# A hybrid GLA/MLA decoder trunk: another rule for the order of its instructions, and MLA's rotary scores as two stacked 128-row products with the mask on TensorE

## The chip, the cores and the metric

The kernel runs on one core of one Trainium2 chip. The metric is the device time of one execution in microseconds (us). TensorE (PE) multiplies matrices, VectorE (DVE) and ScalarE (ACT) work elementwise, GpSimd (POOL) helps, SyncE (SP) issues most of the transfers from HBM.

## What is computed

Two layers; layer 0 mixes tokens with gated linear attention (GLA), layer 1 with multi-head latent attention (MLA). Each layer is a feed-forward half-step, the mixer with four heads of attention to a memory of 256 tokens, and a second feed-forward half-step. All is float32, 512 tokens of width 1024.

```python
for i in range(DEPTH):                                   # DEPTH = 2
    x = x + 0.5 * swiglu(rmsnorm(x, ...), ...)           # d_ff 2816
    h = rmsnorm(x, mix_norm[i])
    # i = 0: gated linear attention, 4 heads;  i = 1: MLA, 8 heads
    o, o_mem = token_mixer(h), memory_cross_attention(q_mem, rmsnorm(mem), ...)
    x = x + concat([o, o_mem]) @ w_out[i]
    x = x + 0.5 * swiglu(rmsnorm(x, ...), ...)

def mla_attention(c_q, c_kv, k_r, ...):
    q  = (rmsnorm(c_q)  @ w_uq ).reshape(B, S, 8, 128 + 64)
    kv = (rmsnorm(c_kv) @ w_ukv).reshape(B, S, 8, 128 + 128)
    q_nope, q_rope = rmsnorm(q[..., :128]), apply_rope(rmsnorm(q[..., 128:]), cos, sin)
    k_nope, v      = rmsnorm(kv[..., :128]), kv[..., 128:]
    k_rope = apply_rope(rmsnorm(k_r), cos, sin)          # one key of 64 for all heads
    s = (q_nope @ k_nope.T + q_rope @ k_rope.T) * 192 ** -0.5
    return softmax(where(causal, s, -inf)) @ v           # in blocks of 128 queries
```

## The kernel before

**Numbers as two parts.** The weights and most activations go to TensorE as a high part, rounded to the format fp32r, and a low part, the rest; a product is then three fp32r products (`mm3`: high by high, high by low, low by high). The profile prints these as f32 too; they are the ones whose operands are tiles `wh` and `wl` (the parts of a weight). ACT makes the high part of a weight (`wh<-raw`), DVE the low part (`wl<-raw,wh`). Products inside the two attentions of a mixer, with operands in tiles `t` only, are mostly plain float32: such a product is one row in the program and two records in the trace.

**Flows and their order.** The program has no order written out by hand. Every piece of work is a Python generator (a flow) that yields one instruction after the other; `Flows.run` takes, again and again, the flow whose next instruction could start first, and emits that instruction to its engine. When it could start is worked out from a table of prices (`Engine.price`: a duration and a latency for each operation) and from the times at which the tiles' blocks were written and read. Among equal starts the lower `rank` goes first: 2 for the trunk (all weight products of TensorE in their fixed order), 1 for most helpers, 0 for the urgent ones (attention chains, copies out of PSUM), and for the splitting of weights -1 or 3, as few or enough weights lie ready. So the order on each engine follows from the prices; the time on the chip does not enter it.

**MLA.** After the latents (`latents`, one for each of four token blocks) and the memory's projections, four pairs of heads follow. For each pair the trunk projects keys and values, then queries, from the latents. `query` copies 384 columns of a block out of PSUM (two heads of 128, two rotary parts of 64) and sums their squares; `queries` makes the inverse roots with `newton_rsqrt`, 13 DVE instructions on 16 columns, of which most read what the one ahead wrote; it scales the blocks, rotates the rotary parts on POOL (`rotate`), and transposes three blocks of 128 for each token block. The two heads' rotary parts share one block: head 0 in rows 0 to 63, head 1 in rows 64 to 127. `keys` does the same for the keys, and `rope_key` makes the one rotary key, written twice, in rows 0 to 63 and 64 to 127.

`attend` takes one head. For each block `j` of 128 queries it makes scores of `n = 128 (j + 1)` columns, with two float32 products into one bank:

```python
yield T.matmul(ps[:, :n], lhsT=st["q"][i][:, sl], rhs=st["k"][i][:, :n], start=True, stop=False)
yield T.matmul(ps[:, :n], lhsT=st["q"][2][rp, sl], rhs=kr["t"][rp, :n], start=False, stop=True)
```

The second, over the 64 rows `rp` of its head, is the rotary product: 8 heads by 4 blocks, 32 in all. In `attention` DVE then adds the causal mask to the last 128 columns (`ps<-ps,cm`), takes the maximum, ACT takes the exponential, DVE the reciprocal and the scaling; four transposes at most, a copy by ACT, and the products with the values end the block's chain. At most two blocks of a head run at the same time.

Of the kernel before, what the change touches and what calls it, by code (L numbers as in the profile page):

```python
# [9 lines left out]
F32 = mybir.dt.float32  # L10
# [39 lines left out]
for _part in (  # L50
# [3 lines left out]
    (("rows", QR + KVR + 2 * ROPE), ("cmask", P), ("cos", NJ * 32), ("sin", NJ * 32), ("invn", 3), ("invq", 16)),  # L54
# [67 lines left out]
class Engine:  # L122
# [19 lines left out]
    def price(self, method, kw, outs, ins):  # L142
# [22 lines left out]
class Flows:  # L165
# [11 lines left out]
    def used(self, name, lo, hi):  # L177
        return max([0.0] + [d.get((name, b), 0.0) for d in (self.wr, self.rd) for b in range(lo // BLOCK, hi // BLOCK)])
# [45 lines left out]
    def start(self, op):  # L224
        t = self.clock.get(op.eng, 0.0)
        for r in op.reads:
            t = max(t, self.wr.get(r, 0.0))
        for w in op.writes:
            if op.eng != "PE":
                t = max(t, self.wr.get(w, 0.0))  # L230
            t = max(t, self.rd.get(w, 0.0))
        return t

# [30 lines left out]
    def run(self):  # L264
        while True:
# [12 lines left out]
            (at, _, _), f = best  # L278
# [6 lines left out]
            for w in op.writes:  # L285
                self.wr[w] = max(self.wr.get(w, 0.0), end + op.lat)
# [3 lines left out]
def _emit(tc, ctx, xT, memT, wflat, sizes, cst, out):  # L290
# [816 lines left out]
    def attention(scores, blocks, value, o, mask=None):  # L1107
# [265 lines left out]
    def rotate(dst, src, tabs, n):  # L1373
# [7 lines left out]
        yield G.tensor_tensor(out=dst[:, :, 0:32], in0=a, in1=b, op=ALU.subtract)  # L1381
        yield G.tensor_tensor(out=a2, in0=t1, in1=s1, op=ALU.mult)
        yield G.tensor_tensor(out=b2, in0=t2, in1=c2, op=ALU.mult)
        yield G.tensor_tensor(out=dst[:, :, 32:64], in0=a2, in1=b2, op=ALU.add)
        done(tmp)

    def mla(l, nrm, nxt):
# [6 lines left out]
        yield from rope_tables(rt)  # L1394
        spawn(mem_prep(l, mem.mp))
# [41 lines left out]
        def rope_key():  # L1437
# [10 lines left out]
            kr["t"] = yield tt()  # L1448
            yield A.copy(out=kr["t"], in_=ps)
# [14 lines left out]
        def query(st, j, ps):  # L1464
# [6 lines left out]
            yield V.tensor_reduce(out=ss[:, 4 * j : 4 * j + 2], in_=heads(sq[:, :256], 2), op=ALU.add, axis=AX.X)  # L1471
            yield V.tensor_reduce(out=ss[:, 4 * j + 2 : 4 * j + 4], in_=heads(sq[:, 256:384], 2), op=ALU.add, axis=AX.X)
# [4 lines left out]
        def queries(st):  # L1477
            for f in st["f"]:
                yield f
            ss, rc = st["ss"], small(16)  # L1480
            yield V.tensor_tensor(out=ss, in0=ss, in1=C("invq"), op=ALU.mult)
            yield from rsqrt(rc, ss, 1.0, 16)
            st["q"] = []
            for _ in range(3):
                st["q"].append((yield tt()))
            q0, q1, qr = st["q"]
            for j in range(NJ):
                qn = st["raw"][j]
                for c0, c1, dd, cc in ((0, 256, NOPE, 4 * j), (256, 384, ROPE, 4 * j + 2)):
                    q3 = heads(qn[:, c0:c1], 2)  # L1490
                    yield V.tensor_tensor(out=q3, in0=q3, in1=rc[:, cc : cc + 2].unsqueeze(2).to_broadcast([P, 2, dd]),
                                          op=ALU.mult)
                tabs = [rt[i][:, j, :].unsqueeze(1).to_broadcast([P, 2, 32]) for i in range(4)]
                yield from rotate(heads(qn[:, 384:512], 2), heads(qn[:, 256:384], 2), tabs, 64)
            for j in range(NJ):
                qn = st["raw"][j]
                pt = yield bank()
                for i, c0 in enumerate((0, 128, 384)):
                    yield T.transpose(out=pt[:, i * P : (i + 1) * P], in_=qn[:, c0 : c0 + P], identity=ident)
                done(qn)  # L1500
                sl = slice(j * P, (j + 1) * P)
                for i in range(2):
                    yield A.activation(out=st["q"][i][:, sl], in_=pt[:, i * P : (i + 1) * P], func=AF.Identity, scale=qns)
# [302 lines left out]
```

## Time and profile before

| | |
|---|---|
| median of three runs | 2018.34 us |
| lowest and highest of them | 2017.01 and 5475.93 us |
| the profiled execution | 2016.53 us, of which the span is 2014.7 us |
| PE, busy share of the span | 99% |
| DVE, ACT, POOL | 78%, 49%, 2% |
| granted clock of TensorE | 1.00 |
| HBM | 189.05 MB read, 95 GB/s over the span |

The profile shows one execution, from the first instruction to the last (the span); 1.8 us of the execution lie around it. All instructions carry the line 138 of a helper that emits them, so groups are told apart by tile names and shapes: `ps` a PSUM bank, `t` a working tile, `s` a small one, `cs` the first block of constants (the identity for transposes stands there), `cm` the constants of a mixer (the mask). By its instructions the span falls into the feed-forward of layer 0 (to about 365 us), GLA (to 622), the two feed-forwards between the mixers (to 1390), MLA with its output projection (to about 1640) and the last feed-forward.

### The profile page before, as it was taken

The page shows a single profiled execution, that of the slowest core. Times are in us where ns is not written, and L with a number is a line of the kernel's source. Part 1 is how long each engine was busy: PE and PEld are TensorE (multiplying, and loading weights), DVE is VectorE, ACT ScalarE, POOL GpSimd, SP SyncE. Part 2 cuts the span into 40 slices and gives each one's busy share as a digit, 9 for nine tenths or more (in the row PEclk, how much of TensorE's full clock was granted, in tenths as well). Part 3 has the DMA queues.
Part 4 walks back from the last instruction along what each step waited for, and adds up shares of the span by engine and source line. Part 5 has one row for each costly group of instructions (what it writes and reads, how often), then busy time and mean ns, then how long its engine had stood idle before and what let it go on. Part 6 is the DMA issues. An engine that isn't in the chain of part 4 may idle for free.

```text
span 2014.7 us, 32006 instructions
## 1 busy us (share of the span) xinstructions
PE 1999.7 (99%) x12862; PEld 1796.6 (89%) x12862; DVE 1578.5 (78%) x2573; ACT 978.3 (49%) x1574; POOL 48.4 (2%) x121
## 2 busy tenths in 40 slices
PE   9999999999999999999999999999999999999999
PEld 8999998878987899999899999989877779998997
DVE  8977786548776998678799777865887669987782
ACT  6543444444442664445565444444576456543451
POOL 0000000000000000000000000010031100000000
PEclk9999999999999999999999999999999999999999
DMA  5333333313212133323323333333210212332231
GB/s 180 108 108 102 105 105 112 108 63 105 74 57 79 64 97 114 115 86 104 126 96 105 105 105 100 101 115 111 87 45 32 84 43 84 105 128 92 95 126 63
DMA packets 55589, 193.22 MB, mean 96 GB/s; under 512 B 6160, under 2 KB 7824, under 8 KB 55440
## 3 DMA queue, kind: packets, MB, share of 16 engines
q1 hardware_dynamic: 55152, 189.92, 28.6%
q8 instruction: 101, 1.65, 0.3%
q10 hardware_dynamic: 288, 1.26, 0.2%
q14 instruction: 48, 0.39, 0.1%
HBM read 189.05 MB, written 2.10 MB: 95 GB/s over the span
## 4 chain that ended last, share of the span: by engine, by line
PE 87%; DVE 9%; ACT 2%; issue 1%; DMA 0%; POOL 0%; SPq 0%; ACTq 0%; DVEq 0%; POOLq 0%
PE ps L138 87%; DVE t L138 5%; DVE wl L138 2%; DVE s L138 2%; ACT t L138 1%; ACT wh L138 1%; DMA raw<-wflat 0%; DVE raw L138 0%; DVE x L138 0%; POOL t L138 0%; SPq L138 0%; DVE ps L138 0%; DVE rs L138 0%; ACTq L138 0%; DVEq L138 0%
## 5 line engine op out<-in xcount | busy, mean ns | idle before, releaser
L138 PE MATMUL ps<-t,wh 128*128 128x256 f32 (+1 forms) x6880 | 1528.0, 318 | 2.8 <-ACT wh L138 1.7
L138 PEld LDWEIGHTS ps<-t,wh 128*128 128x128 f32 x6880 | 1141.1, 191 | 96.0 <-issue 7.2
L138 PE MATMUL ps<-t,wl 128*128 128x256 f32 (+1 forms) x3440 | 1091.1, 317 | 0.1
L138 PEld LDWEIGHTS ps<-t,wl 128*128 128x128 f32 x3440 | 655.5, 191 | 45.6 <-issue 3.0
L138 ACT CAST wh<-raw 128x1024 fp32r<-128x1024 f32 (+2 forms) x358 | 368.6, 1031 | 483.8 <-PE ps L138 357.1
L138 DVE TENSOR_TENSOR wl<-raw,wh 128x1024 fp32r<-128x1024 f32 (+2 forms) x358 | 428.4, 1199 | 114.3 <-ACT wh L138 113.6
L138 DVE TENSOR_TENSOR t<-t 128x512 f32<-128x512 f32 (+3 forms) x514 | 306.5, 618 | 13.1 <-ACT t L138 8.4
L138 ACT CAST wh<-t 128x1024 fp32r<-128x1024 f32 x126 | 132.4, 1051 | 185.5 <-PE ps L138 98.9
L138 PE MATMUL ps<-wh,t 128*128 128x256 f32 (+3 forms) x928 | 214.9, 321 | 0.0
L138 DVE TENSOR_TENSOR wl<-t,wh 128x1024 fp32r<-128x1024 f32 x126 | 153.7, 1220 | 48.9 <-ACT wh L138 48.8
L138 DVE SCALAR_TENSOR_TENSOR x<-ps,x 128x512 f32<-128x512 f32 x160 | 109.8, 686 | 104.7 <-PE ps L138 104.6
L138 ACT COPY t<-ps 128x512 f32<-128x512 f32 (+3 forms) x262 | 138.8, 534 | 65.1 <-PE ps L138 58.5
L138 PEld LDWEIGHTS ps<-wh,t 128*128 128x128 f32 x928 | 155.1, 190 | 9.6 <-issue 2.2
L138 DVE TENSOR_TENSOR t<-ps,t 128x512 f32<-128x512 f32 (+2 forms) x191 | 122.6, 645 | 50.3 <-PE ps L138 36.0
L138 PE MATMUL ps<-wl,t 128*128 128x256 f32 (+3 forms) x464 | 148.2, 319 | 0.0
L138 PE MATMUL ps<-t 128*128 128x128 f32 (+6 forms) x760 | 139.7, 328 | 0.8 <-ACT t L138 0.4
L138 ACT CAST t<-t 128x256 fp32r<-128x256 f32 (+1 forms) x196 | 95.3, 509 | 78.8 <-DVE t L138 78.5
L138 PEld LDWEIGHTS ps<-t 128*128 128x128 f32 (+1 forms) x760 | 97.9, 190 | 30.4 <-issue 15.9
L138 DVE SCALAR_TENSOR_TENSOR t<-t 128x512 f32<-128x512 f32 (+1 forms) x168 | 106.0, 636 | 16.9 <-ACT t L138 16.2
L138 DVE TENSOR_TENSOR t<-t,raw 128x1024 f32<-128x1024 f32 x84 | 102.2, 1217 | 0.1
L138 ACT ACTIVATE t<-t 128x512 f32<-128x512 f32 x124 | 76.3, 629 | 48.1 <-DVE t L138 47.8
L138 PEld LDWEIGHTS ps<-wl,t 128*128 128x128 f32 x464 | 88.3, 190 | 4.9 <-issue 0.9
(76 smaller groups left out, 786.4 us busy)
## 6 DMA issues: line engine op xcount, KB each, us to landing
raw<-wflat SPq DMA_DIRECT2D x342, 512.0 KB, 3.3
raw<-wflat SPq DMA_DIRECT2D x12, 192.0 KB, 2.3
x<-xT SPq DMA_DIRECT2D x8, 256.0 KB, 5.6
t<-memT SPq DMA_DIRECT2D x8, 256.0 KB, 3.6
out<-x SPq DMA_DIRECT2D x8, 256.0 KB, 2.0
raw<-wflat SPq DMA_DIRECT2D x4, 448.0 KB, 3.3
cm<-cst ACTq DMA_DIRECT2D x1, 640.0 KB, 3.9
cm<-cst ACTq DMA_DIRECT2D x1, 585.5 KB, 4.2
```

What stands on the lines that cost most here:

```text
L138: return Op(self.name, lambda: real(*args, **kw), cost, _places(ins), _places(outs), lat)
```

## The change

It has two halves.

**The order.** ACT is priced 95 ns more for each pointer operand and for an accumulated sum, POOL higher. An instruction that reads what the same engine wrote (not on PE) counts no latency any more; before, it counted the latency whatever the engine. And a flow's start is handicapped by 60 ns for each rank above 0 when the next flow is chosen.

**MLA.** Each head's rotary query of 64 columns is split into a high and a low part, which lie side by side, so that their transpose is one tile of 128 rows (`st["qr"]`, high in rows 0 to 63, low in 64 to 127). The rotary key, twice 64 rows as before, is split into a high tile and a low tile. The rotary score is then two fp32r products of 128 rows, by the key's high tile and by its low tile. The mask is a third fp32r product, of an identity and the mask in fp32r (`exact`, made once), on the last 128 columns; DVE's add goes. In `query` one sum over six groups of 64 takes the place of two sums; in `queries` one scaling the place of two, and the nope heads' sums are made from two halves each and written twice (three small instructions); `rotate` issues its four products ahead of the difference and the sum. Four blocks instead of three are transposed for each token block, and the copies behind the transposes take both heads in one instruction.

```diff
         if self.name == "ACT":
-            return 100 + 0.833 * n, 130
+            pointers = sum(_is_ap(kw.get(k)) for k in ("scale", "bias"))
+            return 100 + 0.833 * n + 95 * pointers + 95 * _is_ap(kw.get("accum_out")), 130
         if self.name == "POOL":
-            return 100 + 2.2 * n, 200
+            return 100 + 2.8 * n, 250
...
         for r in op.reads:
-            t = max(t, self.wr.get(r, 0.0))
+            t = max(t, self.written(r, op))
...
+    def written(self, r, op):
+        at, lat, eng = self.wr.get(r, (0.0, 0.0, None))
+        return at if eng == op.eng and eng != "PE" else at + lat
...
-                    k = (self.start(f[3]), f[0]() if callable(f[0]) else f[0], f[1])
+                    rank = f[0]() if callable(f[0]) else f[0]
+                    k = (self.start(f[3]) + 60 * max(rank, 0), rank, f[1], self.start(f[3]))
...
-            if mask is not None:
-                sl = slice(j * P, (j + 1) * P)
-                yield V.tensor_tensor(out=ps[:, sl], in0=ps[:, sl], in1=mask, op=ALU.add)
...
-            kr["t"] = yield tt()
-            yield A.copy(out=kr["t"], in_=ps)
+            kr["t"] = yield from pair()
+            yield from split(ps, *kr["t"])
...
-            yield V.tensor_reduce(out=ss[:, 4 * j : 4 * j + 2], in_=heads(sq[:, :256], 2), op=ALU.add, axis=AX.X)
-            yield V.tensor_reduce(out=ss[:, 4 * j + 2 : 4 * j + 4], in_=heads(sq[:, 256:384], 2), op=ALU.add, axis=AX.X)
+            yield V.tensor_reduce(out=ss[:, 6 * j : 6 * j + 6], in_=heads(sq[:, :384], 6), op=ALU.add, axis=AX.X)
...
+                qh, ql = (heads(qn[:, 256:], 2)[:, :, i * ROPE : (i + 1) * ROPE] for i in range(2))
+                yield from rotate(ql, heads(qn[:, 256:384], 2), tabs, 64)
+                yield A.copy(out=qh.bitcast(F32R), in_=ql)
+                yield V.tensor_tensor(out=ql, in0=ql, in1=qh, op=ALU.subtract)
...
-                for i, c0 in enumerate((0, 128, 384)):
-                    yield T.transpose(out=pt[:, i * P : (i + 1) * P], in_=qn[:, c0 : c0 + P], identity=ident)
+                yield from transposes(pt, qn)
...
-                yield T.matmul(ps[:, :n], lhsT=st["q"][2][rp, sl], rhs=kr["t"][rp, :n], start=False, stop=True)
+                for part in range(2):
+                    yield T.matmul(ps[:, :n], lhsT=st["qr"][:, i * S + j * P : i * S + n], rhs=kr["t"][part][:, :n],
+                                   start=False, stop=False, skip_group_check=True)
+                yield T.matmul(ps[:, sl], lhsT=identr, rhs=maskr, start=False, stop=True, skip_group_check=True)
```

Two places show how the instructions stand now. The first is PE, where the scores of the first pair of heads begin. Before: bank 14697 holds head 0's first block, 14698 its second, 14699 and 14700 those of head 1; `t_13090` is the rotary key.

```order
L138 MATMUL ps_14697<-t_14243,t_9731 128x128
L138 MATMUL ps_14697<-t_13090,t_14216 128x128
L138 MATMUL ps_14698<-t_14243,t_9731 128x256
L138 MATMUL ps_14698<-t_13090,t_14216 128x256
L138 MATMUL ps_14699<-t_14275,t_14147 128x128
L138 MATMUL ps_14699<-t_13090,t_14216 128x128
L138 MATMUL ps_14700<-t_14275,t_14147 128x256
L138 MATMUL ps_14700<-t_13090,t_14216 128x256
```

Now, for head 0's first two blocks (banks 14685 and 14686): `t_13414` and `t_13709` are the key's high and low tile, `t_13107` holds the identity and the mask.

```order
L138 MATMUL ps_14685<-t_14265,t_14368 128x128
L138 MATMUL ps_14685<-t_13414,t_14369 128x128
L138 MATMUL ps_14685<-t_13709,t_14369 128x128
L138 MATMUL ps_14685<-t_13107 128x128
L138 MATMUL ps_14686<-t_14265,t_14368 128x256
L138 MATMUL ps_14686<-t_13414,t_14369 128x256
L138 MATMUL ps_14686<-t_13709,t_14369 128x256
L138 MATMUL ps_14686<-t_13107 128x128
```

Two rows for each block have become four, of which three are fp32r. The second place is DVE in `latents`, where the inverse roots of the four token blocks are made, each in small tiles of its own. Before, three of them took turns (13427 and 13428, 13433 and 13434, 13444 and 13445):

```order
L138 SCALAR_TENSOR_TENSOR s_13428<-s_13427 128x3
L138 SCALAR_TENSOR_TENSOR s_13445<-s_13444 128x3
L138 SCALAR_TENSOR_TENSOR s_13433<-s_13434,s_13433 128x3
L138 TENSOR_TENSOR s_13428<-s_13428,s_13426 128x3
L138 TENSOR_TENSOR s_13445<-s_13445,s_13443 128x3
L138 SCALAR_TENSOR_TENSOR s_13434<-s_13433 128x3
L138 SCALAR_TENSOR_TENSOR s_13427<-s_13428,s_13427 128x3
L138 SCALAR_TENSOR_TENSOR s_13444<-s_13445,s_13444 128x3
```

Now the first block's root runs through by itself, with one weight's low part between:

```order
L138 TENSOR_TENSOR s_13432<-s_13432,s_13430 128x3
L138 SCALAR_TENSOR_TENSOR s_13431<-s_13432,s_13431 128x3
L138 SCALAR_TENSOR_TENSOR s_13432<-s_13431 128x3
L138 TENSOR_TENSOR s_13432<-s_13432,s_13430 128x3
L138 SCALAR_TENSOR_TENSOR s_13431<-s_13432,s_13431 128x3
L138 TENSOR_TENSOR wl_13418<-raw_13240,wh_13417 128x1024
L138 SCALAR_TENSOR_TENSOR s_13432<-s_13431 128x3
L138 TENSOR_TENSOR s_13432<-s_13432,s_13430 128x3
L138 SCALAR_TENSOR_TENSOR s_13403<-s_13432,s_13431 128x3
```

Nearly every row now reads what the row ahead of it wrote. Counted over the whole order of DVE, that holds for 450 of 2538 instructions now and for 358 of 2575 before; 65 of the 92 more stand between the 348th and the 372nd weight's low part, which the trace of before has from about 1400 to 1516 us. The order of the weights' transfers on SP is the same, and so is the trunk's on PE.

More of the change, by code (lines that the diff above doesn't have):

```diff
@@ L177, in used @@
     def used(self, name, lo, hi):
-        return max([0.0] + [d.get((name, b), 0.0) for d in (self.wr, self.rd) for b in range(lo // BLOCK, hi // BLOCK)])
+        keys = [(name, b) for b in range(lo // BLOCK, hi // BLOCK)]
+        return max([0.0] + [self.rd.get(k, 0.0) for k in keys] + [sum(self.wr[k][:2]) for k in keys if k in self.wr])
     def done(self, *tiles):
@@ L1104, in _emit, with attention @@
     xqs = const.tile([P, 2], F32, name="xqs")
-    def attention(scores, blocks, value, o, mask=None):
+    def attention(scores, blocks, value, o):
         po = yield bank(1)
@@ L1479, in queries @@
                 yield f
[L1480 to L1486, printed above, removed]
+            ss, rc = st["ss"], sm.tile([P, 24], F32, tag="s6", name="s6", bufs=8)
+            two = ss.rearrange("p (j b) -> p j b", j=NJ)[:, :, :4].rearrange("p j (h b) -> p j h b", h=2)
+            sums = small(8)
+            yield V.tensor_tensor(out=sums.rearrange("p (j h) -> p j h", j=NJ), in0=two[:, :, :, 0], in1=two[:, :, :, 1],
+                                  op=ALU.add)
+            for b in range(2):
+                yield V.tensor_scalar_mul(out=two[:, :, :, b], in0=sums.rearrange("p (j h) -> p j h", j=NJ), scalar1=0.5)
+            v, y, t = (sm.tile([P, 24], F32, tag="s6", name="s6", bufs=8) for _ in range(3))
+            yield from newton_rsqrt(rc, ss, 1.0 / ROPE, v, y, t)
+            st["q"] = yield Take("d", F32, 0)
+            st["qr"] = yield Take("d", F32R, 0)
             for j in range(NJ):
                 qn = st["raw"][j]
[L1489 to L1492, printed above, removed]
+                q3 = heads(qn[:, :384], 6)
+                yield V.tensor_tensor(out=q3, in0=q3, in1=rc[:, 6 * j : 6 * j + 6].unsqueeze(2).to_broadcast([P, 6, ROPE]),
+                                      op=ALU.mult)
                 tabs = [rt[i][:, j, :].unsqueeze(1).to_broadcast([P, 2, 32]) for i in range(4)]
-                yield from rotate(heads(qn[:, 384:512], 2), heads(qn[:, 256:384], 2), tabs, 64)
+                qh, ql = (heads(qn[:, 256:], 2)[:, :, i * ROPE : (i + 1) * ROPE] for i in range(2))
+                yield from rotate(ql, heads(qn[:, 256:384], 2), tabs, 64)
+                yield A.copy(out=qh.bitcast(F32R), in_=ql)
+                yield V.tensor_tensor(out=ql, in0=ql, in1=qh, op=ALU.subtract)
             for j in range(NJ):
@@ L1522, in keys @@
             yield from rsqrt(rc, st["ks"], 1.0 / NOPE, 8)
-            st["k"] = []
-            for _ in range(2):
-                st["k"].append((yield tt()))
+            st["k"] = yield Take("d", F32, 0)
             for j in range(NJ):
@@ L1532, in keys @@
                 sl = slice(j * P, (j + 1) * P)
-                for i in range(2):
-                    yield A.activation(out=st["k"][i][:, sl], in_=pt[:, i * P : (i + 1) * P], func=AF.Identity,
-                                       scale=C("kn"))
+                yield A.activation(out=heads(st["k"], 2)[:, :, sl], in_=heads(pt[:, : 2 * P], 2), func=AF.Identity,
+                                   scale=C("kn"))
                 done(pt)
@@ L1780, in _pack_consts @@
     put("invn", np.broadcast_to(np.array([1.0 / QR, 1.0 / KVR, 1.0 / ROPE], np.float32), (P, 3)))
-    put("invq", np.broadcast_to(np.tile(np.array([1 / NOPE, 1 / NOPE, 1 / ROPE, 1 / ROPE], np.float32), 4), (P, 16)))
     return c
```

32 lines of the change are left out of this document (18 added, 14 removed).

## The prediction

> **What bounds the kernel now.** I read the page's first part, then the busy time by stage, then what ends the waits in the stage that changes.
>
> ```profile
> span 2014.7 us, 32006 instructions
> PE 1999.7 (99%) x12862; PEld 1796.6 (89%) x12862; DVE 1578.5 (78%) x2573; ACT 978.3 (49%) x1574; POOL 48.4 (2%) x121
> ```
>
> PE is busy 1999.7 of 2014.7 us: 15.0 us idle are all that a better order could give back of what the page calls idle. The stages, with PE's busy time as the second number and DVE's as the fourth:
>
> ```profile
> 365.00:622.00 257.00, 256.26 (x1535) 214.83 (x1535) 177.79 (x370) 107.87 (x187) 2.04 (x4) 1.00 0.23 77
> 622.00:1390.00 768.00, 766.76 (x5151) 712.24 (x5150) 627.62 (x809) 373.05 (x522) 5.89 (x8) 1.00 0.31 103
> 1700.00:2014.00 314.00, 310.39 (x2112) 288.86 (x2110) 236.34 (x275) 134.41 (x167) 0.00 (x0) 1.00 0.31 100
> ...
> 1400.00:1495.00 95.00, 90.04 (x525) 78.15 (x524) 85.38 (x324) 61.31 (x159) 22.22 (x53) 1.00 0.27 81
> 1495.00:1640.00 145.00, 143.79 (x768) 107.48 (x768) 96.81 (x281) 78.75 (x218) 16.95 (x50) 1.00 0.15 48
> ```
>
> In the feed-forwards between the mixers PE idles 1.2 of 768 us, in GLA 0.7 of 257. There the time is that of the trunk's products, which the change leaves as they are; DVE has 140 us to spare in the 768, so a moved weight split or copy stays covered. The last row of feed-forward idles 3.6 us, mostly the end. One stretch stands out: the opening of MLA, 1400 to 1495 us, where PE idles 5.0 us while DVE is busy 85.4 of 95. The chain of work through it and one of its waits:
>
> ```profile
> by line: PE ps L138 36.4%; DVE s L138 24.6%; DVE wl L138 12.3%; DVE t L138 9.3%; issue 5.9%; ACT t L138 4.2%; ACT wh L138 3.2%; POOL t L138 3.2%; DVE ps L138 0.9%; ACTq L138 0.1%; POOLq L138 0.0%; DVEq L138 0.0%
> ...
> 1477.20 0.41 PE L138 MATMUL ps<-cs,t 128*128 128x128 f32 x2 [1.33 <-DVE t L138]
> ```
>
> Nearly half of that chain (24.6 + 12.3 + 9.3 + 0.9%) is DVE, and PE stands 1.33 us before a transpose that DVE's scaling of the keys releases. So two prices matter: what TensorE's products in MLA cost, and what DVE needs in MLA's opening.
>
> **PE: the rotary product that goes.** These are the 32 products over 64 rows, two records each, from 1480 to 1630 us:
>
> ```profile
> L138 PE MATMUL ps<-t 64*128 64x512 f32 x16 | 9.0, 641 | 0.0
> L138 PE MATMUL ps<-t 64*128 64x384 f32 x16 | 7.3, 535 | 0.0
> L138 PE MATMUL ps<-t 64*128 64x256 f32 x16 | 5.6, 428 | 0.0
> L138 PE MATMUL ps<-t 64*128 64x128 f32 x16 | 3.9, 322 | 0.0
> ...
> 1499.44 1.44 PE L138 MATMUL ps<-t 128*128 128x128 f32 x4
> 1500.81 0.33 PE L138 MATMUL ps<-cs,t 128*128 128x128 f32 x1
> ```
>
> Together 25.8 us busy. Busy time counts the drain of a product, over which the next may run, so it can be too much; the timeline's group tells. Its four records are two short ones of 128 columns and one rotary product of 512 (the group prints its first shape), and the next group starts 1.37 us after it. With 0.12 us for each short one (below), 1.13 us are left for the product, as 9.0 / 8 = 1.13. So the drain is not covered here, and I take **-25.8 us**. The other end: an fp32r product of 512 lasts 0.39 us and the next starts after 0.23 (next rows), so at most 0.16 us of each is covered, 32 x 0.16 = 5.1, which leaves -20.7.
>
> **PE: what comes.** Starts of neighbouring fp32r products, of 512, 384 and 256 columns:
>
> ```profile
> 1478.61 0.39 PE L138 MATMUL ps<-wl,t 128*128 128x512 f32 x1
> 1478.84 0.62 PE L138 MATMUL ps<-wh,t 128*128 128x512 f32 x2
> ...
> 1481.93 0.34 PE L138 MATMUL ps<-wl,t 128*128 128x384 f32 x1
> 1482.11 0.52 PE L138 MATMUL ps<-wh,t 128*128 128x384 f32 x2
> ...
> 1300.22 0.28 PE L138 MATMUL ps<-t,wl 128*128 128x256 f32 x1
> 1300.34 0.40 PE L138 MATMUL ps<-t,wh 128*128 128x256 f32 x2
> ```
>
> That is 0.23, 0.18 and 0.12 us. No row has an fp32r product of fewer than 256 columns, and 48 of the new ones have 128 (16 rotary, 32 mask). They are bounded by
>
> ```profile
> L138 PE MATMUL ps<-ones,t 128*128 128x1 f32 x20 | 2.4, 237 | 0.0
> L138 PE MATMUL ps<-t 128*128 128x128 f32 x176 | 27.4, 283 | 0.0
> L138 PE MATMUL ps<-cs,t 128*128 128x128 f32 x180 | 30.5, 276 | 2.5 <-ACT t L138 1.8 <-DVE t L138 0.5
> ```
>
> Even one column costs 2.4 / 20 = 0.12 us, as much as 256 columns of fp32r, so 0.12 is the lower end. The upper end is plain float32 of this width: two records of 27.4 / 176 = 0.156, 0.31 us. I take 0.12, since 256 columns of the same format already cost no more. The sum: 16 x (0.23 + 0.18 + 0.12 + 0.12) = 10.4 for the rotary products and 32 x 0.12 = 3.8 for the mask, **+14.2 us**; by the upper end 48 x 0.19 = 9.1 more. Sixteen more transposes, at 30.5 / 180 = 0.17, are **+2.7 us**. PE's own work: -25.8 + 14.2 + 2.7 = **-8.9 us**, with ends -8.9 and -20.7 + 14.2 + 9.1 + 2.7 = +5.3. PE is the bound through this stage (143.8 of 145 us), so I count all of it.
>
> [...]
>
> ```profile
> 438.87 0.70 PE L138 MATMUL ps<-t 64*128 64x256 f32 x4
> 439.50 0.50 PE L138 MATMUL ps<-t,wh 128*128 128x512 f32 x1
> ```
>
> Two products of 256 columns in the two halves take 0.63 us from start to next start; in MLA one takes 5.6 / 8 = 0.70. If MLA's two heads paired up like that, half of 25.8 would have been saved already, and PE's work would change by -12.9 + 14.2 + 2.7 = +4.0. But in the order of before a full-height product stands between any two rotary ones, and their busy rows show no pairing. [...]
>
> **DVE and ACT.**
>
> ```profile
> L138 DVE TENSOR_TENSOR ps<-ps,cm 128x128 f32<-128x128 f32 x32 | 9.5, 295 | 9.4 <-PE ps L138 9.0
> L138 DVE TENSOR_TENSOR t<-t,s 128x256 f32<-128x256 f32 x20 | 8.9, 458 | 0.1
> L138 DVE TENSOR_TENSOR t<-t,s 128x128 f32<-128x128 f32 x12 | 4.1, 338 | 0.0
> L138 DVE TENSOR_REDUCE s<-t 128x2 f32<-128x256 f32 x15 | 6.2, 411 | 1.5 <-ACT t L138 1.5
> L138 DVE TENSOR_REDUCE s<-t 128x2 f32<-128x128 f32 x8 | 2.2, 276 | 0.0
> L138 DVE TENSOR_REDUCE s<-ps 128x1 f32<-128x384 f32 x8 | 4.4, 553 | 0.1
> L138 ACT ACTIVATE t<-ps,qns 128x128 f32<-128x128 f32 x32 | 10.2, 386 | 8.3 <-PE ps L138 8.1
> L138 ACT ACTIVATE t<-ps,s 128x256 f32<-128x256 f32 x24 | 11.4, 479 | 5.1 <-DVE s L138 5.0
> ```
>
> The mask's 32 adds, 9.5 us, leave DVE, and 0.3 us leaves each block's chain. Joined sums save 0.41 + 0.28 - 0.55 = 0.14 us for each of 16 blocks, 2.2; joined scalings 0.46 + 0.34 - 0.58 (extended by 0.12 for each 128 columns) = 0.22, 3.5. The new subtraction costs about 0.34 a block, 5.4; the wider copy out of PSUM and three small instructions for each pair about 4. So DVE is about 6 us lighter over MLA, but the mask falls late: before the first scores, at about 1486 us, it is about even. ACT's joined copies save 2 x 0.39 - 0.48 = 0.29 us, 32 times (queries and keys), 9 us, less 16 casts of about 0.3. I cost these at nothing for the end, since PE covers them from 1495 on; where cover fails, a chain is 0.3 us shorter for the mask, and a query block about 0.6 longer for the cast and the subtraction.
>
> **The order.** What the new prices leave out can be seen in four rows of DVE's timeline:
>
> ```profile
> 1475.37 0.15 DVE L138 TENSOR_TENSOR s<-s 128x8 f32<-128x8 f32 x1
> 1475.44 0.27 DVE L138 TENSOR_REDUCE s<-t 128x2 f32<-128x128 f32 x1
> ...
> 1480.75 0.17 DVE L138 SCALAR_TENSOR_TENSOR s<-s 128x16 f32<-128x16 f32 x1
> 1480.95 0.17 DVE L138 TENSOR_TENSOR s<-s 128x16 f32<-128x16 f32 x1
> ```
>
> A small instruction is followed after 0.07 us by one that does not need its result, and after 0.20 by one that does. The old price had a latency for the second case and put other work between; the new one does not, and 92 more instructions stand right behind the one whose result they read, 65 of them between 1400 and 1516 us. At 0.13 us that is 8.5 us of DVE in the stretch where DVE is 90% busy, and queued behind them are the weights' low parts, the scalings and so PE's transposes. DVE idles 9.6 us there, which absorbs some, and the first block of each kind is ready sooner. I take a third of 8.5 for PE, **+2.8 us**, with ends 0 and 8.5. The handicap of 60 ns lets PE wait up to 0.12 us for an urgent helper; better prices for ACT place helpers nearer to their operands. Both work in the mixers alone; their balance I put at nothing, and the gain at no more than the idle of MLA, 5.0 + 1.2 = 6.2 us.
>
> **The sum**, against the profiled execution's 2016.53 us (span 2014.7): -8.9 + 2.8 = -6.1, **2010.4 us**. The median of the three runs is 2018.34 and the lowest 2017.01, so the profiled one is a usual one.
>
> **The rivals.**
> - *The order repays.* MLA's idle time goes, as chains finish sooner and nothing is lost to the tighter rows: 2016.5 - 8.9 - 6.2 = 2001.4. For it speaks that PE waits for helpers there and that ACT's rows with pointers (0.386 us for 128 columns) lie above their old price; against it DVE's load.
> - *DVE's opening gets slower.* All 92 tight pairs reach PE, 92 x 0.13 = 12.0 us: 2016.5 - 8.9 + 12.0 = 2019.6, slower than before. Place: latents to the first scores, 1400 to 1495 us. It decides once more than 8.9 of the 12.0 us arrive at PE, which needs the opening's DVE slack to be gone.
> - *The narrow products run as float32*, so the change does not do there what it says: 2010.4 + 9.1 = 2019.5. No row excludes it.
> [...]
>
> **How the numbers follow.** Forecast 0.50, order repays 0.22, DVE's opening 0.13, narrow products 0.13, pairing 0.02. The range reaches from the first rival less 3 us for the end of PE's own waits that no row calls idle to the two slower ones and 3.5 us for both of them in part: 1998 to 2023. Two per cent of the median, about what a measurement of this kernel can tell from no change, are 40 us. No case comes near: faster than 1978 would need more than all idle time and the whole rotary product, slower than 2059 several times the loss of any rival. I leave 0.01 and 0.02 for what I have not seen, and 0.97 within.
>
> **What will show it.** The 64-row shapes of MLA are gone, and PE's groups of `ps<-t` with 128 rows grow by 48 records of 128 columns that start 0.12 us after each other (0.31 would be the third rival). PE's busy time is 8 to 9 us lower, and its idle time from 1400 to 1495 us a little higher than 5.0. DVE's busy time is about 6 us lower, but DVE's instructions on `s` in the latents stand 0.20 us apart throughout. The feed-forward stages keep their length within 1 us. I am wrong if those stages move, since then the order touches more than the mixers, or if PE's idle time in MLA passes 12 us.

## The result, and the profile after

The changed kernel takes 2038.84 us (median of four runs, 2036.88 to 2041.55) against 2017.67 before: a ratio of 1.0106, 95% interval 1.0089 to 1.0124. The prediction was 2010.4, with a range of 1998 to 2023. It is 21 us slower, outside the range, on the side of the cases that the prediction's chances call DVE's opening, narrow products and pairing, 0.28 together; it is within the two per cent of the median for which the prediction gave 0.97. The profiled execution took 2036.88 us.

The page after, span and engines:

```profile
span 2035.1 us, 32011 instructions
PE 1997.9 (98%) x12910; PEld 1809.6 (89%) x12910; DVE 1585.2 (78%) x2536; ACT 977.8 (48%) x1558; POOL 46.3 (2%) x121
```

PE's idle time is 37.2 us where it was 15.0, and its busy time is only 1.8 us lower. The stages after, with PE's busy time as the second number and the granted clock in front of the last two:

```profile
365.00:622.00 257.00, 256.09 (x1535) 215.26 (x1534) 179.24 (x369) 105.98 (x186) 2.05 (x4) 1.00 0.24 78
622.00:1390.00 768.00, 767.23 (x5149) 712.42 (x5148) 630.02 (x812) 373.83 (x522) 5.89 (x8) 1.00 0.32 103
1400.00:1495.00 95.00, 84.14 (x482) 73.65 (x482) 81.64 (x306) 52.10 (x126) 13.46 (x37) 0.95 0.25 76
1495.00:1640.00 145.00, 127.11 (x773) 107.28 (x772) 96.83 (x279) 83.60 (x227) 23.64 (x67) 0.95 0.11 37
1720.00:2034.00 314.00, 311.35 (x2124) 290.24 (x2122) 237.52 (x275) 134.21 (x168) 0.00 (x0) 1.00 0.31 103
```

GLA and both feed-forward stages are as before. All of the loss lies in MLA: PE idles 10.9 us of 95 and 17.9 of 145, and the granted clock is 0.95 where it was 1.00. Over one window for all of MLA, 1390 to 1660 us, which the experiments below use, the two kernels read, before and after:

```profile
1390.00:1660.00 270.00, 263.54 (x1460) 211.72 (x1459) 205.14 (x679) 155.87 (x408) 39.17 (x103) 1.00 0.19 60
```

```profile
1390.00:1660.00 270.00, 241.25 (x1426) 207.47 (x1425) 190.33 (x610) 143.11 (x368) 37.10 (x103) 0.96 0.18 57
```

PE's idle time there goes from 6.5 to 28.8 us. What PE waits for in that window, and the wait on ACT that before does not have (total, times, longest):

```profile
PE ps L138 <- DVE t L138: 21.5, 9, 5.8
PE ps L138 <- ACT t L138: 5.0, 5, 3.3
PE ps L138 <- POOL t L138: 2.0, 1, 2.0
...
ACT t L138 <- POOL t L138: 17.2, 11, 2.9
```

The 21.5 us are a few long stops, each at a transpose (`ps<-cs,t` reads the identity). PE's timeline, with the wait in brackets:

```profile
1463.54 0.41 PE L138 MATMUL ps<-cs,t 128*128 128x128 f32 x2 [2.39 <-DVE t L138]
...
1485.35 0.66 PE L138 MATMUL ps<-cs,t 128*128 128x128 f32 x2 [5.85 <-DVE t L138]
...
1506.49 0.45 PE L138 MATMUL ps<-cs,t 128*128 128x128 f32 x1 [4.51 <-DVE t L138]
...
1561.50 0.30 PE L138 MATMUL ps<-cs,t 128*128 128x128 f32 x1 [3.28 <-ACT t L138]
1576.67 1.88 PE L138 MATMUL ps<-cs,t 128*128 128x128 f32 x9 [4.11 <-DVE t L138]
1590.44 0.41 PE L138 MATMUL ps<-cs,t 128*128 128x128 f32 x2 [3.52 <-DVE t L138]
```

The longest, 5.85 us, can be followed through the helpers' timelines of after:

```profile
1471.92 0.18 DVE L138 TENSOR_TENSOR s<-s,s 128x24 f32<-128x24 f32 x1
1472.13 0.18 DVE L138 SCALAR_TENSOR_TENSOR s<-s,s 128x24 f32<-128x24 f32 x1
...
1473.22 2.21 DVE L138 TENSOR_TENSOR t<-t,s 128x384 f32<-128x384 f32 x4
...
1473.94 8.60 POOL L138 TENSOR_TENSOR t<-t 128x64 f32<-128x64 f32 x24 [55.37 <-DVE t L138]
...
1475.36 1.34 DVE L138 TENSOR_TENSOR wl<-raw,wh 128x1024 fp32r<-128x1024 f32 x1
...
1477.47 0.30 ACT L138 CAST t<-t 128x128 fp32r<-128x128 f32 x1 [2.88 <-POOL t L138]
...
1477.80 0.35 DVE L138 TENSOR_TENSOR t<-t 128x128 f32<-128x128 f32 x1 [1.10 <-ACT t L138]
1478.08 0.42 DVE L138 TENSOR_REDUCE s<-t 128x2 f32<-128x256 f32 x1
1479.12 0.55 DVE L138 TENSOR_REDUCE s<-t 128x6 f32<-128x384 f32 x1 [0.61 <-ACT t L138]
1479.59 0.16 DVE L138 TENSOR_SCALAR s<-s 128x8 f32<-128x8 f32 x1
...
1484.59 0.16 DVE L138 SCALAR_TENSOR_TENSOR s<-s 128x8 f32<-128x8 f32 x1
...
1484.78 1.43 DVE L138 TENSOR_TENSOR t<-t,s 128x256 f32<-128x256 f32 x4
```

The queries' inverse roots (DVE, `s<-s,s`) end at 1473 us. POOL rotates. ACT's new cast stands 2.88 us in the middle of ACT's queue until POOL has done the first block, and behind it are the squares and copies that the next sums need. DVE's new subtraction waits 1.10 us for that cast. Behind it in DVE's order come the keys' last sum (1478.08), a sum of the next queries (1479.12), which waits 0.61 us for ACT, and only then the keys' inverse root on 8 columns: its 13 instructions, with other work between them, run from 1479.59 to 1484.75. The keys' scaling comes at 1484.78, and PE, which has stood at that transpose since 1479.5, goes on at 1485.35. PE's order is fixed by the plan, and in the 5.85 us the trace has nothing on PE of what stands behind the transpose. From 1470 to 1487 us the chain of waits is 38.3% DVE's `s` and 19.5% POOL.

The same root takes as long in before:

```profile
1471.21 0.29 DVE L138 TENSOR_SCALAR s<-s 128x8 f32<-128x8 f32 x1
...
1476.10 0.15 DVE L138 SCALAR_TENSOR_TENSOR s<-s 128x8 f32<-128x8 f32 x1
...
1476.65 0.41 DVE L138 TENSOR_TENSOR t<-t,s 128x256 f32<-128x256 f32 x1
```

That is 5.0 us against 5.2. But there PE came to the transpose when the root was nearly done, and stood 1.33 us (the row of 1477.20 in the prediction); in after it came there before the root had begun. What changed is the place of the transpose in PE's order against the chain of the helpers.

The stops of 4.51, 4.11 and 3.52 us are of another kind: they stand before transposes of attention blocks, which DVE's softmax scaling releases (`t<-t,s`, TENSOR_SCALAR). DVE's rows of after ahead of them:

```profile
1503.23 0.29 DVE L138 TENSOR_TENSOR t<-t 128x128 f32<-128x128 f32 x1 [1.01 <-ACT t L138]
...
1506.07 0.27 DVE L138 TENSOR_SCALAR t<-t,s 128x128 f32<-128x128 f32 x1
...
1575.06 1.20 DVE L138 TENSOR_TENSOR wl<-raw,wh 128x1024 fp32r<-128x1024 f32 x1
1576.18 1.13 DVE L138 TENSOR_SCALAR t<-t,s 128x256 f32<-128x256 f32 x4
...
1587.92 0.34 DVE L138 TENSOR_TENSOR t<-t 128x128 f32<-128x128 f32 x1 [1.46 <-ACT t L138]
...
1589.63 0.34 DVE L138 TENSOR_TENSOR t<-t 128x128 f32<-128x128 f32 x1 [1.08 <-ACT t L138]
1589.89 0.40 DVE L138 TENSOR_SCALAR t<-t,s 128x256 f32<-128x256 f32 x1
```

Ahead of the first and the third, the split's subtraction stood in DVE's queue and waited for ACT's cast; ahead of the second, DVE made three low parts of weights.

After such stops PE was often slow for a while. The same view of windows, with the granted clock third from the end, in the 5 us after the 5.85 us wait, the next 5 us, and 6 us around the 4.51 us wait:

```profile
1485.00:1490.00 5.00, 4.65 (x17) 3.73 (x18) 3.28 (x15) 2.55 (x9) 0.00 (x0) 0.66 0.29 98
1490.00:1495.00 5.00, 5.00 (x30) 4.31 (x29) 3.94 (x16) 2.64 (x8) 1.92 (x6) 1.00 0.01 3
1506.00:1512.00 6.00, 5.15 (x16) 4.09 (x17) 4.39 (x16) 2.69 (x10) 1.76 (x5) 0.50 0.00 0
```

Over MLA that is 270 x (1 - 0.96) = 10.8 us of full-speed time beside the idle time. It is a rounded figure, and it counts the low clock inside the stops too, where nothing is lost twice: by the clock's records in the trace 23.9 us ran at half rate, some 5 of them inside stops, which leaves about 9.5 us.

### The profile page after: what moved, and what is told of

Read it like the earlier page. It is cut to its first block, busy times and chain, and to the rows that moved or that the text cites. A ratio compares the mean times of both kernels' runs of the same rounds, so it can differ in the third digit from the quotient of the medians.

```text
span 2035.1 us, 32011 instructions
## 1 busy us (share of the span) xinstructions
PE 1997.9 (98%) x12910; PEld 1809.6 (89%) x12910; DVE 1585.2 (78%) x2536; ACT 977.8 (48%) x1558; POOL 46.3 (2%) x121
## 4 chain that ended last, share of the span: by engine, by line
PE 86%; DVE 9%; ACT 2%; issue 1%; POOL 1%; DMA 0%; SPq 0%; POOLq 0%; ACTq 0%; DVEq 0%
PE ps L138 86%; DVE t L138 5%; DVE wl L138 2%; DVE s L138 2%; ACT t L138 2%; POOL t L138 1%; ACT wh L138 1%; DMA x<-xT 0%; DVE x L138 0%; SPq L138 0%; ACT L138 0%; POOLq L1813 0%; ACTq L138 0%; POOLq L138 0%; DVE raw L138 0%
## 5 line engine op out<-in xcount | busy, mean ns | idle before, releaser
L138 DVE TENSOR_TENSOR t<-t 128x512 f32<-128x512 f32 (+4 forms) x530 | 310.3, 608 | 18.2 <-ACT t L138 14.7
L138 ACT CAST t<-t 128x256 fp32r<-128x256 f32 (+2 forms) x212 | 99.5, 494 | 91.7 <-DVE t L138 73.2
L138 PE MATMUL ps<-t 128*128 128x128 f32 (+5 forms) x792 | 134.4, 321 | 1.9 <-ACT t L138 1.4
L138 PEld LDWEIGHTS ps<-t 128*128 128x128 f32 (+1 forms) x792 | 106.0, 194 | 21.1 <-ACT t L138 7.3
```

The lines of the kernel that those rows point to most:

```text
L138: return Op(self.name, lambda: real(*args, **kw), cost, _places(ins), _places(outs), lat)
```

## The experiments

All ratios are against the kernel before, on the same chip, with 95% intervals; changes of less than 0.1% are about what they resolve. "Idle" is PE's idle time from 1390 to 1660 us (before 6.5, after 28.8). Two theories came first. **Q**: MLA's new split makes ACT and DVE wait for POOL inside their queues. **O**: the order's new rule places instructions badly.

**The change in two halves.** The first run has MLA as changed and the order's rule as before; the second the new rule with MLA as before (all hunks of the diff inside `Engine.price` and `Flows`).

> MLA as changed, the order's rule as before. Theory Q (queues): the split of the rotated query makes ScalarE wait for GpSimd and VectorE for ScalarE in the middle of their queues (17.2 us of ScalarE's waits for GpSimd in MLA, none before), which delays keys, sums and weights behind them, and TensorE stands before transposes; the loss belongs to the new MLA under any rule: 2030 us or more. Theory O (order): the new rule for the order is to blame, since it holds dependent instructions of an engine for free; without it TensorE's lighter work comes through: about 2009 us.

> The order's rule as changed, MLA as before. Theory Q: without the split no queue waits for GpSimd, 2012 to 2020 us. Theory O: the loss is here, about 2035 to 2045 us.

```profile
1390.00:1660.00 270.00, 252.73 (x1492) 217.47 (x1491) 196.66 (x632) 150.74 (x385) 37.50 (x103) 0.98 0.19 60
```

```profile
1390.00:1660.00 270.00, 258.40 (x1428) 207.26 (x1427) 201.34 (x665) 150.48 (x398) 36.80 (x103) 0.99 0.19 61
```

New MLA alone: 2021.19 us, 1.0020 [1.0010, 1.0029], idle 17.3 us. New rule alone: 2025.46, 1.0039 [1.0025, 1.0054], idle 11.6. Both halves lose, by 4.2 and 8.4 us, and together they lose 21.8 and not 12.6 (2038.84 against the 2017.04 that before took beside these runs). Neither theory alone holds. The interaction of some 9 us had to be found.

**The split's high part on DVE**, so that no ACT instruction stands behind POOL:

```diff
-                yield A.copy(out=qh.bitcast(F32R), in_=ql)
+                yield V.tensor_copy(out=qh.bitcast(F32R), in_=ql)
```

> The changed kernel, with the high part of the rotated query made by VectorE in place of ScalarE, so that only VectorE's queue waits for GpSimd. Theory Q: ScalarE's waits for GpSimd (17.2 us) go and part of the loss with them, about 2025 us, unless VectorE's own wait takes their place. Theory O: no difference, 2037 to 2041 us.

```profile
1390.00:1660.00 270.00, 246.49 (x1457) 211.21 (x1456) 193.49 (x634) 144.46 (x360) 33.10 (x103) 0.97 0.19 59
```

2030.45 us, 1.0068 [1.0051, 1.0085]. ACT's wait for POOL falls from 17.2 to 0.7 us and the time by 8.4; DVE, which had no such wait, now waits 11.6 us for POOL. Theory Q is a part, not the whole. The same edit under the rule before is told below.

**No stacked product at all**: the changed kernel with the rotary product of before (64 rows, float32, no split, three transposes).

> The changed kernel with the rotary product as before (one float32 product over 64 rows, no split of the rotated query, three transposes); the mask on TensorE, the joined copies and sums and the new rule stay. Theory Q: without the split the waits for GpSimd are gone; TensorE has some 9 us more work than the changed kernel, and still 2015 to 2022 us. Theory O: the loss stays and the work comes on top, about 2045 us.

```profile
1390.00:1660.00 270.00, 255.24 (x1397) 202.68 (x1396) 183.81 (x592) 139.48 (x350) 37.49 (x103) 0.96 0.18 55
```

2038.25 us, 1.0110 [1.0086, 1.0135]: no better. This misled me at first into ruling the split out. Without the split PE idles 14.8 us instead of 28.8, so 14.0 come back. But over the span PE is busy 17.0 us longer (2014.9 against 1997.9, at a granted clock of 0.995 and 0.994), and the rotary products of before, which it does again, are the larger part of that. The two cancel, so the run does not clear the split.

**Which line of the new rule.** First the latency of a result on the same engine is counted again; then, in another run, the handicap of 60 ns for each rank is taken out.

```diff
-        return at if eng == op.eng and eng != "PE" else at + lat
+        return at + lat
```

```diff
-                    k = (self.start(f[3]) + 60 * max(rank, 0), rank, f[1], self.start(f[3]))
+                    k = (self.start(f[3]), rank, f[1], self.start(f[3]))
```

> The changed kernel with one line of the order's rule undone: a result on the same engine counts with its latency again, so dependent small DVE rows are pulled apart; handicap and the new prices stay. If the latency rule is the part of the order that costs (theory L), most of the 8.4 us that the order alone cost (2025.5 against 2017.0) come back: 2028 to 2032 us. If the handicap or the prices cost (theory H), or MLA's new split alone (theory Q), it stays within 3 us of 2038.8.

> The changed kernel without the 60 ns for each rank in the key that picks the next flow; latency rule and prices stay. Theory H: the handicap lets helpers in front of which PE waits go late or early, and without it 4 to 8 us come back, 2031 to 2035. Theories L and Q: within 3 us of 2038.8.

With the latency back: 2022.23 us, 1.0026 [1.0017, 1.0036], idle 16.8. Without the handicap: 2029.74, 1.0064 [1.0048, 1.0079]. The latency line alone carries 16.6 of the 21.8 us, twice what was expected of it.

**MLA's half in parts, under the rule before.** New MLA with the split on DVE; and new MLA with neither stacked product nor split, only the mask on TensorE and the joined copies and sums.

> MLA as changed, the order's rule as before, and the high part of the rotary columns made by DVE instead of ACT, so that no ACT instruction stands behind POOL's rotation. With ACT's cast this measured 2021.2 us, and ACT stood 14.0 us behind POOL. Theory Q (ACT's queue is what costs): the wait on PE shrinks and PE's saved work shows, 2012 to 2018 us, and ACT waits under 2 us for POOL. Rival: DVE is the loaded engine there and 16 more of its instructions cost what ACT's wait cost, 2020 to 2023.

> The order's rule as before, the rotary scores as before (64-row float32 products, no split), with only the mask on TensorE and the joined copies and sums. PE's own work grows by the mask, 32 x 0.12 = 3.8 us. Theory Q (the split's waits are the loss of MLA's part): no new waits, 2017 + 3.8 = 2020 to 2022. If joined tiles and sums cost waits by themselves: 2024 or more, with PE's idle in MLA well over 6.5 us. If they help chains: under 2019.

The first: 2019.07 us, 1.0007 [0.9998, 1.0016], not to be told from before; ACT has no wait of a tile for POOL left, but PE still idles 15.4 us, more than the expectation's gain allowed. The second: 2022.84, 1.0027 [1.0017, 1.0037], idle 6.6: no new waits, and 0.8 us above the expected range. PE's busy time is 5.9 us longer (2005.6 against 1999.7). The clock (0.999) takes about 2 us of that and the masks 1.9 by the price measured below; the other 2 us are not explained.

**Whose latency.** The line undone for POOL alone, and for DVE alone; then both the latency and the handicap undone, so that of the new rule only the prices stay; and the last with the split on DVE.

```diff
-        return at if eng == op.eng and eng != "PE" else at + lat
+        return at if eng == op.eng and eng not in ("PE", "POOL") else at + lat
```

> The changed kernel, with a result on the same engine counted with its latency again on POOL alone; on DVE and ACT the new rule stays. With it back on all engines the kernel measured 2022.2 us against 2038.8. Theory LP: the plan prices a POOL step of a rotation at 279 ns where the trace has 358, and the 250 ns of latency were the margin that hid this; without them ACT's cast and PE's transposes are placed before the rotation can be done. Then nearly all of the 16.6 us come back here: 2022 to 2027. Theory LD (the prediction's own term: dependent small DVE rows stand tight and delay DVE's queue): 2034 to 2039.

> The changed kernel, with a result on the same engine counted with its latency again on DVE alone. Theory LD: 2022 to 2027 us, and DVE's dependent rows of a root are 0.20 us apart less often. Theory LP: 2034 to 2039. Both in part: around 2030 in each of the two.

> The changed kernel with both the same-engine latency back and the handicap of 60 ns for each rank taken out: of the new rule only the prices of ACT's pointers and of POOL stay. The two undone one at a time gave 16.6 and 9.1 us back. If the two act apart (theory A): 2038.8 - 25.7 = 2013 us. If they act on the same waits (theory B), little beyond the larger one: 2018 to 2022, which is where MLA alone with the order before stands (2021.2).

> As the run with the prices only, and the high part of the rotary columns made by DVE, which took 8.4 us off under the new rule and 2.1 us under the rule before. If what is left of MLA's waits is ACT behind POOL: 2 us or more under the run with the prices only, 2011 to 2018; faster than before if PE's idle time from 1390 to 1660 us falls under 12. Otherwise: the same as the run with the prices only, since DVE takes on what ACT loses.

POOL's back: 2026.98 us, 1.0045 [1.0031, 1.0058]. DVE's back: 2023.24, 1.0027 [1.0016, 1.0037]. That is 11.9 and 15.6 of the same 16.6 us: either one does most of it, though they touch different instructions. So neither "DVE's tight rows" nor "POOL's price" is the cause by itself. What they share, I concluded, is the plan's length of the chains that end at a transpose: roots on DVE, rotation on POOL, split. Prices only: 2024.31, 1.0033 [1.0021, 1.0045], so the handicap, worth 9.1 us with the latency gone, is worth nothing once the latency is back; both theories' ranges were missed. With the split on DVE: 2020.07, 1.0011 [1.0003, 1.0020], 4.2 us less, but above its range, and PE still idles 17.4 us.

**Only the transposes moved.** This makes a third theory, PP: the plan takes the helper chain for finished before it is, and so sets PE's transposes too early in PE's fixed order. It is tested by changing nothing else in the plan's rules: a transpose (the only op with a cost of 110) may start 1 us later after its operand was written, and 2 us in a second run. All prices stay as in the change. The order of the other engines can still move with the transposes, and in the traces some of it does.

```diff
-        return at if eng == op.eng and eng != "PE" else at + lat
+        return at if eng == op.eng and eng != "PE" else at + lat + (1000 if op.eng == "PE" and op.cost == 110 and eng else 0)
```

> The changed kernel, in whose plan a transpose of TensorE may start 1 us later after what it reads was written; DVE's and POOL's instructions, their prices and the rule for one engine stay as in the change. Theory PP (placement: the plan takes the chain over DVE, POOL and ACT for finished before it is, and PE's fixed order then parks PE at a transpose): PE's waits for DVE's tiles fall under 3 us each, 2018 to 2027 us. Theory SL (DVE's and POOL's tight rows are themselves slower and everything ends later): 2034 to 2040.

> As the run before, with 2 us. Theory PP: as good as 1 us or better, 2015 to 2025, until tiles held longer cost again. Theory SL: 2034 or more, and more than with 1 us.

```profile
1390.00:1660.00 270.00, 253.98 (x1492) 218.86 (x1491) 200.67 (x633) 151.09 (x385) 36.12 (x103) 0.97 0.19 60
```

With 1 us: 2020.22 us, 1.0015 [1.0005, 1.0024]. 18.6 of the 21.8 us are gone, and PE's waits for DVE's tiles fall from 21.5 to 9.0 us, though one of 5.7 stays. DVE is busy 1582.0 us, nearly as long as in the change (1585.2), so its tight rows are mostly left. With 2 us: 2025.68, 1.0042 [1.0029, 1.0056], just above its range. Theory SL alone is out: moving transposes in the plan brings the time back while DVE's tight rows stay. How much of the gain is the change's own loss needs the same margin on the kernel before.

**The same cure on the other versions.** New MLA under the rule before with the split on DVE, and the kernel before itself, both with 1 us.

> MLA as changed, the order's rule as before, the split's high part on DVE (2019.1 us without more), and transposes planned 1 us later after their operands. PE's idle time from 1390 to 1660 us was 15.4 us there. Theory PP: half of it goes, 2010 to 2015, the first version under the kernel before. Otherwise 2017 to 2021.

> The kernel before with transposes planned 1 us later, to tell whether this helps any kernel. PE idles 6.5 us from 1390 to 1660 us there. Theory PP: little to gain where the plan is nearly right, 2014 to 2018. If 1 us costs something by itself (tiles held longer, PE's products moved away): 2019 or more.

```profile
1390.00:1660.00 270.00, 258.76 (x1514) 222.79 (x1514) 206.20 (x666) 153.43 (x381) 37.86 (x103) 0.99 0.19 61
```

```profile
1390.00:1660.00 270.00, 267.92 (x1486) 217.35 (x1485) 210.60 (x693) 160.66 (x418) 38.35 (x103) 1.00 0.20 62
```

New MLA: 2012.68 us, 0.9978 [0.9969, 0.9987]. The kernel before: **2009.40 us, 0.9960 [0.9947, 0.9974]**, the fastest of all that ran and better than its expectation, which had it at 2014 to 2018. One number in the plan gains 8.7 us there, and no version with the new MLA came under that. With it PE idles 2.1 us of 270.

This bounds what theory PP explains. With no margin the change costs 21.8 us; with 1 us it costs 10.8 (2020.22 against 2009.40). So 8.7 of the 18.6 us are a gain that the kernel before makes too, and about half of the change's own loss is gone; the other half stays as PE's idle time (16.0 us in MLA against 2.1) and the clock (0.97 against 1.00).

PE's busy time is 6.9 us lower in the first than in the second (1989.7 against 1996.6), but its idle time over the span is 9.4 us higher (20.5 against 11.1). What is left are two stops, the first before the keys, the second before an attention block:

```profile
1477.47 0.41 PE L138 MATMUL ps<-cs,t 128*128 128x128 f32 x2 [2.12 <-DVE t L138]
...
1492.76 0.45 PE L138 MATMUL ps<-cs,t 128*128 128x128 f32 x1 [3.04 <-DVE t L138]
```

**More margin.** Whether 2 us would cover those two stops as well:

> MLA as changed, the order's rule as before, the split on DVE, transposes planned 2 us later instead of 1 (2012.7 us with 1). What is left there are two waits of PE for the rotated queries, 2.1 and 3.0 us. If 2 us lets the plan cover these as well: 2006 to 2011, level with the kernel before with 1 us (2009.4) or under it. If the new chain over POOL and the split is too long for any place nearby, or tiles held longer cost as much: 2012 to 2020.

> The kernel before with transposes planned 2 us later instead of 1 (2009.4 us with 1). PE idles 2.1 us in MLA with 1 us, so there is no more to gain: 2008 to 2012 if 2 us costs nothing, over 2013 if tiles held longer cost.

New MLA: 2018.15 us, 1.0007 [0.9998, 1.0016]. The kernel before: 2019.94, 1.0013 [1.0004, 1.0022]. Both expectations of no harm missed: 2 us costs 5.5 to 10.5 us against 1 us in all three versions. In the two under the rule before, a good part of it lies outside MLA. GLA in the kernel before, with 1 us and with 2:

```profile
365.00:622.00 257.00, 256.27 (x1540) 215.90 (x1540) 179.95 (x371) 107.71 (x187) 2.25 (x4) 1.00 0.24 78
```

```profile
365.00:622.00 257.00, 251.65 (x1510) 211.88 (x1509) 175.28 (x366) 105.65 (x184) 2.04 (x4) 0.99 0.23 78
```

PE idles 5.4 us there instead of 0.7, and the clock falls. Compared with 2 us in both kernels, the change costs 5.7 us (2025.68 against 2019.94).

## Why the prediction was wrong, point by point

The span grew by 20.4 us: PE's idle time by 22.2, while its busy time fell by 1.8. In the busy time, the lower clock hides what PE's work lost: with some 9.5 us for the clock, the work fell by about 11.

**PE's own work, -8.9: right, as far as the traces can tell, by two errors that cancel.** The 64-row shapes went, and the narrow products run as fp32r (0.22 us busy for a mask product, where the prediction's row of plain float32 has two records of 0.28). The rival in which they run as float32 is out. One mask product in the trace of new MLA with 1 us, busy time and mean ns last:

```profile
L138 PE MATMUL ps<-t 128*128 128x128 f32 x1 | 0.2, 220 | 0.0
```

Products of 512, 384 and 256 columns last 0.16 us longer than their distance to the next start (0.39 and 0.23, 0.34 and 0.18, 0.28 and 0.12 in the prediction's rows), so 0.22 means 0.06, and in the trace the next start comes 0.058 to 0.060 us later in most of the mask products seen (0.058 at 1532.98 us in after). The 48 narrow ones cost 0.06 and not 0.12: 16 x (0.23 + 0.18 + 0.12 + 0.06) = 9.4 and 32 x 0.06 = 1.9. I had taken the row of 256 columns and the one of a single column instead.

The term would then be -25.8 + 9.4 + 1.9 + 2.7 = -11.8. But 25.8 is busy time, and it is too much: in the group read in the prediction, the two short records take 0.32 us by their starts in the trace and not 0.24, which leaves 1.05 us for the product of 512 and not 1.13. By starts the 32 products of before took 23.7 us, and not half of 25.8: GLA's two products at 438.87 us start 0.007 us apart, MLA's stood one behind the other, so the pairing that had 0.02 of the chances is out. And the first fp32r product behind a plain one took longer than priced (0.32 us to the next start at 512 columns, 0.26 at 384, 0.20 at 256). By starts alone the work falls by about 7 us, by PE's busy time less the clock by about 11. The -8.9 lies between.

**"I cost these at nothing for the end, since PE covers them": this step failed.** It counted ACT's and DVE's work in the new split as busy time beside a busy PE. But the split is a step of a chain, roots, rotation, cast, subtraction, transpose, and it stands in two queues in order. The cast that waited 2.88 us for POOL held up what stood behind it on ACT. DVE's subtraction then waited 1.10 us for the cast, with the keys' sums and roots or a softmax scaling behind it. New MLA alone was 4.2 us slower, where the PE term by itself had promised 8.9 less: 13 us were lost there. Moving the cast to DVE gave back 8.4 us under the new rule and about 2 under the old.

**The order at +2.8, with ends 0 and 8.5: the mechanism was wrong, and the size.** I saw in the trace that a dependent small DVE instruction follows after 0.20 us, and took that as DVE's time. It is that too: DVE is 9.8 us busier than with the latency back (1585.2 against 1575.4). But DVE is not the bound. What counts is that the plan now prices such a row at 70 + 1.042 x 24 = 95 ns, where after's rows stand 0.21 apart (1471.92 and 1472.13); with the latency of 110 it had 205 ns, nearly the truth. A POOL step that reads POOL's result went from 441 ns (100 + 2.2 x 64, and a latency of 200) to 279, where 24 steps take 8.60 us, 358 each. That mean hides two cases. The first four of the 24:

```profile
1473.94 2.94 POOL L138 TENSOR_TENSOR t<-t 128x64 f32<-128x64 f32 x4 [55.37 <-DVE t L138]
```

These take 0.73 us each, while DVE runs its scalings and a weight's low part (1473.22 to 1476.70, shown above); the other 20 take 0.28, the plan's own price. So the new price is true for most steps, and the plan knows nothing of what slows the first ones. Whether DVE is the reason no run tests.

The old latencies were a margin over all of this, and they kept PE's transposes late enough; with them gone, PE is parked. That moving the transposes brings time back with DVE's tight rows left shows the place of the transposes to be a cause; the same margin on the kernel before shows it to be about half of the change's loss. I had the row of 0.20 us in hand and read only DVE's delay from it.

**The balance of handicap and prices, put at nothing:** the handicap cost 9.1 us in the changed kernel and about nothing once the latency was back. So it seems to act on the same waits and not to be a second cause.

**The clock was not in the sum.** I counted PE's waits one for one. A stop often cost a second time, by the clock (in 43 of the 75 stops of 1.4 us or more that the last section counts). This is a part of why two halves that lose 4.2 and 8.4 us lose 21.8 together, and not the larger one. In MLA the halves add 10.8 and 5.1 us of idle time, both together 22.3, which is 6.4 more than their sum. By the mean clock of the span (0.997, 0.999 and 0.994) the clock takes 6.1, 2.0 and 12.2 us, which is 4 more.

**The rival on the slower side** had the right place, 1400 to 1495 us, and the wrong mechanism, and its price was bounded at 12.0 us of DVE's time; with the stop of 5.85 us PE's idle time in that stretch grew from 5.0 to 10.9 only, and more of the loss, 17.9 of 145 us idle, came later, where I had written that PE covers everything. **The signs** I had named did their work: PE's idle time in MLA passed 12 us by far, and the feed-forward stages stayed. PE's busy time fell 1.8 us instead of 8 to 9, which is the clock (some 9.5 us, as worked out above). DVE's rose by 6.7 instead of falling by 6, which is the tight rows: with the new MLA and the order as before it fell by 3.8 (1574.7).

What stays open: why a margin of 2 us hurts all three versions (tiles held longer would be one reason, and was not tried apart); the 10.8 us that the change still costs with 1 us; and the exact share of the loss of each of the two halves in the changed kernel, since they act on the same chain. One rival was not tested. No run disturbs the order of the changed kernel by an edit that should do nothing, so part of the 9 to 19 us that the edits of its plan gave back could be the luck of another order.

## What to carry to other kernels

Where a planner fixes the order of a busy engine, a price that is too low on a helper chain is dear: here PE stood up to 5.85 us before one transpose, and nothing planned behind it ran in that time. One that is too high was dear as well here (5.5 to 10.5 us for the second microsecond), so there is a margin to be found by measuring. Before a latency is taken out of such a table as false, compare the whole planned chain with its rows in the trace; a number that is wrong in name may be right in sum. And work on other engines is "covered" only while its end lies ahead of the next instruction in the bound engine's fixed order, which has to be looked up for every step that the change lengthens.

## What the hardware showed that I had not expected

The granted clock fell to half behind stops of a few us (0.50 from 1485.35 to 1488.40 us in after, behind the stop of 5.85 us, and already in that stop from 1481.6 us on), and the length of the stop does not settle it alone. I counted PE's stops in MLA, 1390 to 1660 us, over the twenty traces, each with the clock's records beside it. A stop of 3.43 us or more came with a stretch of half clock in 15 of 15 cases, one of 2.0 to 3.33 us in 17 of 27, and one of 1.4 to 2.0 us in 11 of 33. The kernel before, where the longest stop there is 1.33 us, has no such stretch in MLA. Each stretch lasted 3.41 us or a multiple of it (in after 3.41 three times and 6.83 twice). In after, the 5 us behind the stops of 2.39, 4.11 and 3.52 us show 0.66, which is 3.41 us at half rate, and the stop of 3.28 us left the clock at 1.00. Which stops bring a stretch, no run shows.

One stretch was longer than any in after: with the rotary product of before under the new rule, the profile's records of PE leave no gap, and yet the clock stayed low:

```profile
1565.00:1577.00 12.00, 12.00 (x39) 8.53 (x39) 4.02 (x14) 4.26 (x13) 0.00 (x0) 0.50 0.00 0
```

That is 12 us at half the clock, behind a wait of 1.45 us; by the clock's records the whole stretch lasts 17.07 us, which is 8.5 us of full-speed time. No run here tells why; it is part of why that version was no faster than the changed kernel.
